# Seven-product up projection of an encoder trunk on one Trainium2 core: weight sums by accumulating DMAs instead of VectorE additions, with a new order table

## The chip, the core and the metric

The kernel runs on one core of one Trainium2 chip. The time is device microseconds of one launch, from three runs of the kernel before: 1785.74, 1783.72 and 1784.91, median 1784.91 us. One further execution was taken by the hardware profiler; every row below is from that one. The engines are named as in the profile: PE is TensorE (PEld its weight loads), DVE is VectorE, ACT is ScalarE, POOL is GpSimd, SP is SyncE, which only issues DMAs here.

## What is computed

Two requests (512 and 256 tokens, together 768 rows, D = 1024) pass through two layers. Layer 0 mixes tokens with a chunked gMLP, layer 1 with a Hyena convolution; each runs beside a cross-attention, and each layer ends in a ConvFFN. The part that the change touches is the first half of layer 1's ConvFFN:

```
def conv_ffn(x, w_up, conv_w, conv_b, w_down):
    h = x @ w_up
    gate = dwconv3(h[..., :D_FF], conv_w, conv_b)
    return (jax.nn.gelu(gate) * h[..., D_FF:]) @ w_down
```

with `D_FF = 2816`, so `w_up` is 1024 x 5632. Everything is float32; a product is made of three single products of a high and a low part (`mm3`: high by high, high by low, low by high).

## The kernel before

**Work and its order.** The program is written as one list of instructions by class `Order` (line 92 on). `schedule` plays that list through with a cost for every instruction and a latency for every hand-over between engines, and emits the instructions engine by engine in the order of that play. Among instructions that could start, the one with the lowest rank goes first; the rank is the instruction's place in the program plus an entry of the table `BIAS` (line 42), which is looked up by the part of the program (`up1`, `out1h1`, ...) and the kind (`pe`, `ve` for DVE, ACT and POOL, `dma`, `load` for whatever serves a weight load). On the chip each engine then runs its own list strictly in order and waits on semaphores for the others. All instructions go through one helper line, so the profile names line L365 for nearly all of them and the groups are told apart by the names of tiles.

**Buffers.** Tiles of 4 KB a partition share 27 places (`s4`). On top of that each kind has a limit of its own: `WR = 4` tiles for raw weights (`wr`, and `wt`, the sums), `WS = 10` tiles for split weights (`ws`). A tile can be filled once one of the places of its kind has been given back by the last reader of an older tile. `wload`, which serves the other projections, takes its raw tile from the same four places.

**Layer 1's up projection** (`ffn_seven`, part `up1`). The 22 blocks of 128 columns are taken in 11 pairs. For each pair `seven` is called twice, once for the gate columns (tiles `g`) and once for the others (tiles `u`): 22 calls. A call makes the four products of two column blocks with two token halves and two halves of the contraction by seven products instead of eight (the Strassen-Winograd scheme), each of 4 x 3 matmuls of 128x384, 84 matmuls a call. The seven right sides are the tiles `x`, made once by `seven_of` from three pairs of token tiles when layer 1's output projection is done (part `out1h1`). The seven left sides come from `seven_weights`: two raw tiles R1 and R2 of 128x1024 (a column block each; half a is the first half of the contraction, half b the second), of which products 1 and 2 use the halves of R1 as they are, product 3 uses R2's half b, and

- product 5 uses R1a + R2a,
- product 6 uses R1a + R2a + R2b,
- product 7 uses R2a + R2b,
- product 4 uses R1a + R1b + R2a + R2b.

Before, DVE makes those with four additions of 128x512 (`wt<-wr`, `wt<-wt,wr`, `wr<-wr`, `wr<-wt,wr`), two of them in place in R2 and R1, so a call holds three of the four raw places. Each weight tile is then split: ACT copies it to the high part, DVE subtracts that from it for the low part. A call fills seven `ws` tiles. The raw tiles are loaded by SP. SP's list also holds the stores of the gated rows (`hsp<-gate`), which wait for DVE.

**The output projection before it** (`out_proj`, part `out1`, its second half `out1h1`) finishes one tile of 128 tokens after the other, in the order 0, 3, 1, 4, 2, 5. Each tile is normed (`rpost`, `rstd` on POOL; `xr`, `y` on DVE; squares on ACT), and each pair goes through `seven_of`: four differences on DVE (`sd`, `se`), transposes on PE (`tps`), and the split of `x` on ACT and DVE. POOL does only such small statistics and a few memsets; it runs nothing in the up projection.

Of the kernel before, what the change touches and what calls it, by code (L numbers as in the profile page):

```python
# [13 lines left out]
F32 = mybir.dt.float32  # L14
# [3 lines left out]
ALU = mybir.AluOpType  # L18
# [15 lines left out]
B8, B4 = 14, 27  # L34
T4, WR, WS, M8, M4 = 9, 4, 10, 14, 22
# [3 lines left out]

AHEAD = 427  # L40
BIAS = {
    ('', 'dma'): -2,
    ('att0', 'pe'): -316, ('att0', 've'): -260,
    ('att1', 'pe'): -14, ('att1', 've'): -1384,
    ('block0', 'pe'): -163, ('block0', 've'): -39,
    ('block1', 'load'): 340, ('block1', 'pe'): -167, ('block1', 've'): 145,
    ('block2', 'load'): 1617, ('block2', 've'): -9,
    ('conv', 'dma'): 560, ('conv', 'pe'): -564, ('conv', 've'): -528,
    ('down0', 'load'): 958, ('down0', 'pe'): 163,
    ('down0h0', 've'): -4337,  # L50
    ('down0h1', 'dma'): 2296, ('down0h1', 'pe'): 305, ('down0h1', 've'): -207,
    ('down1', 'load'): 1243, ('down1', 'pe'): -12,
    ('down1h0', 've'): 261,
    ('down1h1', 'dma'): 293, ('down1h1', 've'): -320,
    ('filters', 'dma'): 790, ('filters', 'pe'): 146, ('filters', 've'): 1331,
    ('gate', 'dma'): 137, ('gate', 'pe'): -8, ('gate', 've'): 289,
    ('kv0', 'dma'): -214, ('kv0', 'load'): 897, ('kv0', 'pe'): -937,
    ('kv1', 'dma'): -395, ('kv1', 'load'): -76, ('kv1', 'pe'): -858, ('kv1', 've'): 21,
    ('mixed', 'pe'): -486, ('mixed', 've'): 124,
    ('normv', 've'): -1344,  # L60
    ('out0', 'load'): 532, ('out0', 'pe'): -124,
    ('out0h0', 've'): -1398,
    ('out0h1', 'dma'): 1199, ('out0h1', 'pe'): 67, ('out0h1', 've'): -313,
    ('out1', 'load'): 13, ('out1', 'pe'): -143,
    ('out1h0', 've'): 816,
    ('out1h1', 'dma'): -336, ('out1h1', 'pe'): -113, ('out1h1', 've'): -391,
    ('pre', 'dma'): -1178, ('pre', 'load'): -660, ('pre', 'pe'): -165,
    ('presplit', 'dma'): -820, ('presplit', 've'): -839,
    ('q0', 'pe'): 232, ('q0', 've'): -564,
    ('q1', 'load'): 1748, ('q1', 'pe'): 140, ('q1', 've'): 123,  # L70
    ('rows', 'load'): -821, ('rows', 'pe'): 293, ('rows', 've'): 294,
    ('up0', 'pe'): -154, ('up0', 've'): -1419,
    ('up1', 'dma'): -300, ('up1', 'load'): 324, ('up1', 'pe'): 61, ('up1', 've'): -419,
    ('x2', 'load'): -53, ('x2', 'pe'): -34, ('x2', 've'): 159,
}
LN_EPS = 1e-5
ATT_SCALE = 0.125
# [15 lines left out]
class Order:  # L93
# [57 lines left out]
    def add(self, eng, method, args, kw):  # L151
        i = len(self.ops)
        outs = [kw[k] for k in ("out", "accum_out") if isinstance(kw.get(k), bass.AP)]
        ins = [v for k, v in kw.items() if isinstance(v, bass.AP) and k not in ("out", "accum_out")]
        pos = [v for v in args if isinstance(v, bass.AP)]
        if "out" not in kw:
            outs, ins = outs + pos[:1], ins + pos[1:]
        else:
            ins += pos
        deps, after, tiles = set(), set(), []  # L160
        for write, aps in ((False, ins), (True, outs)):
            for ap in aps:
                name = ap.tensor.name
                dram = ap.space == bass.MemoryType.DRAM
                if dram and name not in self.state:
                    if name not in self.dram:
                        continue
                st = self.state.setdefault(name, ([], []))
                p0, p1, m = self.region(ap)
                if ap.space == bass.MemoryType.PSUM:  # L170
                    p0, p1, m = 0, 128, 1
                for lst in (st if write else st[1:]):
                    for o, e, q0, q1, mm in lst:
                        if p0 < q1 and q0 < p1 and m & mm:
                            deps.add(o)
                if write:
                    for n in range(2):
                        st[n][:] = [x for x in st[n] if not (p0 <= x[2] and x[3] <= p1 and x[4] & ~m == 0)
                                    or x[0] == i]
                    st[1].append((i, eng, p0, p1, m))  # L180
                else:
                    st[0].append((i, eng, p0, p1, m))
                t = self.tiles.get(name)
                if t is not None and t["ops"] and t["ops"][0] != i:
                    after.add(t["ops"][0])
                if t is not None and (not t["ops"] or t["ops"][-1] != i):
                    t["ops"].append(i)
                    tiles.append(name)
        deps.discard(i)
        kind = "load" if self.load else {"tensor": "pe", "sync": "dma"}.get(eng, "ve")  # L190
        self.rank.append(i + BIAS.get((self.part, kind), 0))
        self.ops.append((eng, method, args, kw, deps, tiles, self.cost(eng, method, kw, args, outs, ins), after - deps))

    @staticmethod
    def cost(eng, method, kw, args, outs, ins):
        n = max(int(np.prod([c for s, c in x.ap[1:]])) for x in outs)
        psum = any(x.space == bass.MemoryType.PSUM for x in ins)
        if eng == "tensor":
            if method == "transpose":
                return 110  # L200
            if kw["rhs"].dtype == F32R:
                return 13.5 + n / 2.4 if n >= 256 else 229
            return 20 + 4 * n / 2.4
        if eng == "scalar":
            c = (52 if psum else 95) + 0.833 * n
            return c + (190 if isinstance(kw.get("bias"), bass.AP) or isinstance(kw.get("scale"), bass.AP) else 0) + \
                (90 if "accum_out" in kw else 0)
        if eng == "vector":
            if method in ("tensor_scalar", "tensor_copy") and not psum:
                return 68 + 0.522 * n  # L210
            if method == "tensor_reduce" or method == "bn_stats":
                n = max(int(np.prod([c for s, c in x.ap[1:]])) for x in ins)
            return (130 if method == "scalar_tensor_tensor" else 69) + 1.042 * n
        if eng == "gpsimd":
            return 300 + 1.1 * n if method == "memset" else 600
        return 450


    def schedule(self):
        ops, N = self.ops, len(self.ops)  # L220
# [69 lines left out]
        while oldest < N:  # L290
            best = None
            for e, c in pool.items():
                pick, at = None, None
                skipped = 0
                for i in sorted(c, key=self.rank.__getitem__):
                    if i > oldest + AHEAD:
                        continue
                    t = allowed(i)
# [10 lines left out]
            at, i, e = best  # L309
            pool[e].remove(i)  # L310
            c = ops[i][6]
            if e == "sync":
                ap = ops[i][3]["out"]
                n = 4 * ap.ap[0][1] * int(np.prod([x[1] for x in ap.ap[1:]]))
                start = max(dma_free, at + 1100)
# [20 lines left out]
            for name in ops[i][5]:  # L336
                t = self.tiles[name]
                left[name] -= 1
                t["end"] = max(t["end"], finish[i])
                if left[name] == 0:  # L340
                    for tag, b in t["res"]:
                        ahead[tag].discard(pos[name, tag])
                        free[tag].append(t["end"] + (900 if e == "sync" else 200))
            while oldest < N and done[oldest]:
                oldest += 1
            for tag in ahead:
# [2 lines left out]
            for u, whole in users[i]:  # L349
                if not whole:  # L350
                    ready_t[u] = max(ready_t[u], at + 1)
                lat = self.LAT[e][ops[u][0]]
                if whole:
                    ready_t[u] = max(ready_t[u], finish[i] + lat)
                need[u] -= 1
                if need[u] == 0:
                    pool[ops[u][0]].append(u)
# [70 lines left out]
class Prog:  # L428
# [146 lines left out]
    def seven_weights(self, ap1, ap2):  # L575

        with self.nc.of(load=True):
            R1, R2, T = (self.nc.tile(self.p4, [128, 1024], F32, "s4", B4, n, n, WR) for n in ("wr", "wr", "wt"))
            self.nc.sync.dma_start(out=R1, in_=ap1)
            self.nc.sync.dma_start(out=R2, in_=ap2)  # L580
            a, b = slice(0, 512), slice(512, 1024)
            W = {}

            def split(src, *ms):
# [2 lines left out]
                for m, q in zip(ms, (a, b)):  # L587
                    W[m] = h[:, q], l[:, q]
            split(R1, 1, 2)
            self.tt(T[:, a], R1[:, a], R2[:, a], ALU.add)  # L590
            self.tt(T[:, b], T[:, a], R2[:, b], ALU.add)
            split(T, 5, 6)
            self.tt(R2[:, a], R2[:, a], R2[:, b], ALU.add)
            split(R2, 7, 3)
            self.tt(R1[:, a], T[:, b], R1[:, b], ALU.add)
            w = self.ws([128, 2, 512])
            self.split(w[:, 0], w[:, 1], R1[:, a])
            W[4] = w[:, 0], w[:, 1]
            return W

    def seven(self, ap1, ap2, xc, name):
# [861 lines left out]
```

## Time and profile before

| | |
|---|---|
| median of three runs | 1784.91 us (1783.72 to 1785.74) |
| time of the profiled execution | 1784.29 us |
| its span in the profile | 1782.5 us |
| mean granted PE clock | 0.992 of full |
| PE busy | 1745.7 us, 98% of the span |
| DVE busy | 1143.0 us, 64% |
| ACT busy | 696.3 us, 39% |
| POOL busy | 82.2 us, 5% |
| DMA traffic | 236.19 MB, mean 133 GB/s |

Layer 1's up projection takes the stretch from about 1268 to 1588 us of the span. A time in the profile is counted from the start of the span; "busy" is the time in which at least one instruction of that engine ran. PE's matmuls overlap one another, so the durations of single matmuls add up to more than PE's busy time. In a timeline row, the bracket says how long the engine had been idle before and which engine's result ended that idle time.

### The profile page before, as it was taken

How to read it: one execution, taken by the hardware profiler on the slowest of the kernel's cores; microseconds unless marked ns; L12 is line 12 of the kernel's file. 1: busy time of each engine (PE TensorE's matmuls, PEld its weight loads, DVE VectorE, ACT ScalarE, POOL GpSimd, SP SyncE). 2: the span in 40 equal slices, each digit the busy share in tenths (PEclk: the TensorE clock that was granted, in tenths of full speed). 3: DMA queues.
4: the chain of work that ended last, by engine and by line, in shares of the span. 5: the costliest groups of instructions: out<-in, count | busy, mean ns of one | idle time of the engine just before them, and what ended most of it. 6: DMA issues, size and time to landing. Idle time of an engine off the chain costs nothing.

```text
span 1782.5 us, 23756 instructions
## 1 busy us (share of the span) xinstructions
PE 1745.7 (98%) x9504; PEld 1542.9 (87%) x9504; DVE 1143.0 (64%) x1675; ACT 696.3 (39%) x1075; POOL 82.2 (5%) x165
## 2 busy tenths in 40 slices
PE   7999999999999999999999999999799999999998
PEld 6988878888888888888798888888699999998886
DVE  6464456456545666663656989764988888874352
ACT  6373344333323334552441222554454443443320
POOL 2001020000000000000300000001100000000001
PEclk9999999999999999999999999999799999999999
DMA  7112044122323135786753324123323232356522
GB/s 268 60 65 95 24 171 139 38 97 75 118 90 114 66 134 220 292 315 219 252 213 118 118 83 131 36 95 118 107 77 127 73 127 77 131 209 224 195 81 106
DMA packets 66830, 236.19 MB, mean 133 GB/s; under 512 B 7475, under 2 KB 7679, under 8 KB 64160
## 3 DMA queue, kind: packets, MB, share of 16 engines
q1 hardware_dynamic: 66720, 234.68, 37.4%
q8 instruction: 75, 1.23, 0.3%
q14 instruction: 35, 0.29, 0.1%
HBM read 183.00 MB, written 51.64 MB: 132 GB/s over the span
## 4 chain that ended last, share of the span: by engine, by line
PE 93%; DVE 5%; DMA 1%; issue 1%; ACT 1%; POOL 1%; POOLq 0%; SPq 0%; DVEq 0%; ACTq 0%
PE rp L365 32%; PE fmp L365 10%; PE fma L365 10%; PE fmb L365 10%; PE bQ L365 8%; PE bA L365 5%; PE bP L365 5%; PE dft L365 3%; PE iv L365 1%; PE kps L365 1%; PE vps L365 1%; PE tps L365 1%; PE h L365 1%; PE sc L365 1%; PE pv L365 1%; DVE x L365 1%
## 5 line engine op out<-in xcount | busy, mean ns | idle before, releaser
L365 PE MATMUL fmp<-hTP,ws 128*128 128x256 f32 x1584 | 405.4, 286 | 0.0
L365 DVE TENSOR_TENSOR ws<-wr,ws 128x1024 fp32r<-128x1024 f32 (+1 forms) x192 | 219.7, 1158 | 118.0 <-ACT ws L365 79.6
L365 PE MATMUL fma<-hTS,ws 128*128 128x512 f32 x792 | 290.1, 398 | 1.6 <-DVE hTS L365 0.8
L365 PEld LDWEIGHTS fmp<-hTP,ws 128*128 128x128 f32 x1584 | 288.4, 190 | 3.1 <-issue 1.1
L365 PE MATMUL fmb<-hTS,ws 128*128 128x512 f32 x792 | 290.9, 399 | 0.0
L365 PE MATMUL bQ<-x,ws 128*128 128x384 f32 x792 | 247.6, 334 | 0.0
L365 ACT ACTIVATE ws<-wr 128x1024 fp32r<-128x1024 f32 (+1 forms) x192 | 189.4, 1004 | 147.7 <-DMA wr<-w_up 68.4
L365 PE MATMUL rp<-ws,xs 128*128 128x512 f32 x792 | 185.1, 389 | 0.0
L365 PEld LDWEIGHTS fma<-hTS,ws 128*128 128x128 f32 x792 | 148.8, 188 | 35.0 <-ACT hTS L365 1.4
L365 PEld LDWEIGHTS fmb<-hTS,ws 128*128 128x128 f32 x792 | 148.8, 188 | 33.3
L365 PE MATMUL bP<-x,ws 128*128 128x384 f32 x528 | 176.4, 334 | 0.0
L365 PEld LDWEIGHTS rp<-ws,xs 128*128 128x128 f32 x792 | 148.6, 188 | 30.8
L365 PE MATMUL bA<-x,ws 128*128 128x384 f32 x528 | 171.5, 343 | 1.2 <-DVE x L365 0.8
L365 PEld LDWEIGHTS bQ<-x,ws 128*128 128x128 f32 x792 | 147.1, 188 | 0.3
L365 PE MATMUL rp<-ws,xsS 128*128 128x512 f32 x528 | 136.9, 390 | 0.0
L365 PE MATMUL rp<-ws,mxS 128*128 128x512 f32 x384 | 117.2, 406 | 0.2 <-DVE ws L365 0.2
L365 PEld LDWEIGHTS rp<-ws,xsS 128*128 128x128 f32 x528 | 99.0, 188 | 20.8
L365 PEld LDWEIGHTS bA<-x,ws 128*128 128x128 f32 x528 | 100.5, 192 | 2.4 <-DVE x L365 1.3
L365 PEld LDWEIGHTS bP<-x,ws 128*128 128x128 f32 x528 | 99.1, 188 | 0.2
L365 PEld LDWEIGHTS rp<-ws,mxS 128*128 128x128 f32 x384 | 71.0, 188 | 15.8 <-DVE ws L365 0.5
L365 PE MATMUL rp<-ws,hTS 128*128 128x512 f32 x288 | 83.8, 403 | 0.0
L365 DVE TENSOR_TENSOR xs<-hc,xs 128x1536 fp32r<-128x1536 f32 x22 | 38.6, 1758 | 64.6 <-ACT ws L365 36.6
(255 smaller groups left out, 2695.2 us busy)
## 6 DMA issues: line engine op xcount, KB each, us to landing
wr<-w_up SPq DMA_DIRECT2D x88, 512.0 KB
wr<-w_down SPq DMA_DIRECT2D x44, 512.0 KB
wsp<-pw SPq DMA_DIRECT2D x20, 1024.0 KB
ws<-wsp SPq DMA_DIRECT2D x40, 512.0 KB
hc<-hsp SPq DMA_DIRECT2D x44, 384.0 KB
xs<-xr SPq DMA_DIRECT2D x18, 512.0 KB
praw<-bw SPq DMA_DIRECT2D x18, 512.0 KB
xr<-xs SPq DMA_DIRECT2D x18, 512.0 KB
```

The lines of the kernel that those rows point to most:

```text
L365: getattr(getattr(self.real, eng), method)(*args, **kw)
```

## The change

`seven_weights` makes the sums by DMAs that add to their destination. It takes a fourth tile U, and SP loads four half tiles more per call (R1a into T's half a, R2b into T's half b, R2a into U's half a, R1b into U's half b). Then POOL issues four DMAs from SBUF to SBUF that add: R2a to T's a (product 5), R2b to U's a (product 7), T's a to T's b (product 6), T's b to U's b (product 4). T and U are split as whole tiles, and product 3 is split from R2's half b. The four additions on DVE are gone; the splits are the same in number and size. In `Order`, a DMA that adds counts its destination as an input too, one issued by POOL is costed at 1200 ns of POOL, and its transfer and hand-over like those of a DMA of SP. `BIAS` has new values in nearly all entries, and some entries come and go.

```
 BIAS = {
...
-    ('out1', 'load'): 13, ('out1', 'pe'): -143,
-    ('out1h0', 've'): 816,
-    ('out1h1', 'dma'): -336, ('out1h1', 'pe'): -113, ('out1h1', 've'): -391,
...
+    ('out1', 'load'): -182, ('out1', 'pe'): 289,
+    ('out1h0', 've'): 539,
+    ('out1h1', 'dma'): -1929, ('out1h1', 'pe'): -1500, ('out1h1', 've'): 126,
...
-    ('up1', 'dma'): -300, ('up1', 'load'): 324, ('up1', 'pe'): 61, ('up1', 've'): -419,
-    ('x2', 'load'): -53, ('x2', 'pe'): -34, ('x2', 've'): 159,
...
+    ('up1', 'dma'): -257, ('up1', 'load'): 194, ('up1', 'pe'): -6, ('up1', 've'): 554,
+    ('x2', 'pe'): -24,
 }
...
+        if kw.get("accum_op") is not None:
+            ins.append(kw["out"])
...
+        if eng == "gpsimd" and method == "dma_start":
+            return 1200
...
-            if e == "sync":
+            if e == "sync" or ops[i][1] == "dma_start":
...
-                lat = self.LAT[e][ops[u][0]]
+                lat = self.LAT["sync" if ops[i][1] == "dma_start" else e][ops[u][0]]
...
     def seven_weights(self, ap1, ap2):
         with self.nc.of(load=True):
-            R1, R2, T = (self.nc.tile(self.p4, [128, 1024], F32, "s4", B4, n, n, WR) for n in ("wr", "wr", "wt"))
-            self.nc.sync.dma_start(out=R1, in_=ap1)
-            self.nc.sync.dma_start(out=R2, in_=ap2)
+            R1, R2, T, U = (self.nc.tile(self.p4, [128, 1024], F32, "s4", B4, n, n, WR)
+                            for n in ("wr", "wr", "wt", "wt"))
             a, b = slice(0, 512), slice(512, 1024)
+            put = self.nc.sync.dma_start
+            for o, i in ((R1, ap1), (R2, ap2), (T[:, a], ap1[:, a]), (T[:, b], ap2[:, b]), (U[:, a], ap2[:, a]),
+                         (U[:, b], ap1[:, b])):
+                put(out=o, in_=i)
+            add = lambda o, i: self.nc.gpsimd.dma_start(out=o, in_=i, accum_op=ALU.add)
+            add(T[:, a], R2[:, a])
+            add(U[:, a], R2[:, b])
+            add(T[:, b], T[:, a])
+            add(U[:, b], T[:, b])
             W = {}
...
             split(R1, 1, 2)
-            self.tt(T[:, a], R1[:, a], R2[:, a], ALU.add)
-            self.tt(T[:, b], T[:, a], R2[:, b], ALU.add)
             split(T, 5, 6)
-            self.tt(R2[:, a], R2[:, a], R2[:, b], ALU.add)
-            split(R2, 7, 3)
-            self.tt(R1[:, a], T[:, b], R1[:, b], ALU.add)
+            split(U, 7, 4)
             w = self.ws([128, 2, 512])
-            self.split(w[:, 0], w[:, 1], R1[:, a])
-            W[4] = w[:, 0], w[:, 1]
+            self.split(w[:, 0], w[:, 1], R2[:, b])
+            W[3] = w[:, 0], w[:, 1]
             return W
```

## Rows read from the trace of the kernel before

**Rows 1.** The page, part 1: busy time of each engine.

```profile
PE 1745.7 (98%) x9504; PEld 1542.9 (87%) x9504; DVE 1143.0 (64%) x1675; ACT 696.3 (39%) x1075; POOL 82.2 (5%) x165
```

**Rows 2.** Stretches of 50 us: busy PE, PEld, DVE, ACT, POOL; clock; DMA share; GB/s.

```profile
750.00:800.00 50.00, 50.00 (x222) 41.43 (x221) 33.61 (x35) 28.50 (x40) 2.18 (x2) 1.00 0.88 324
...
1200.00:1250.00 50.00, 46.73 (x221) 38.38 (x219) 24.92 (x34) 19.09 (x40) 8.21 (x19) 1.00 0.30 106
1250.00:1300.00 50.00, 39.40 (x207) 37.45 (x208) 46.98 (x69) 26.08 (x41) 6.57 (x11) 0.80 0.31 106
...
1350.00:1400.00 50.00, 50.00 (x290) 49.99 (x289) 42.44 (x64) 21.73 (x30) 0.00 (x0) 1.00 0.26 87
```

**Rows 3.** Short stretches inside the transition, the same columns.

```profile
1250.00:1255.00 5.00, 0.20 (x1) 0.20 (x2) 5.00 (x8) 2.30 (x4) 2.39 (x4) 0.55 0.52 210
...
1270.00:1275.00 5.00, 5.00 (x20) 4.88 (x19) 4.32 (x7) 2.12 (x2) 0.00 (x0) 0.56 0.49 184
1275.00:1280.00 5.00, 5.00 (x37) 4.83 (x36) 3.81 (x6) 3.30 (x7) 0.00 (x0) 1.00 0.00 0
```

**Rows 4.** Timeline of PE in the transition.

```profile
1254.80 1.97 PE L365 MATMUL tps<-ident,y 128*128 128x128 f32 x8 [8.04 <-DVE y L365]
...
1265.40 1.94 PE L365 MATMUL tps<-ident,y 128*128 128x128 f32 x8 [4.05 <-DVE y L365]
1267.82 1.01 PE L365 MATMUL bA<-x,ws 128*128 128x384 f32 x2 [0.47 <-ACT x L365]
1269.57 4.85 PE L365 MATMUL bA<-x,ws 128*128 128x384 f32 x14 [0.75 <-DVE x L365]
```

**Rows 5.** Timeline of DVE at the start of the up projection.

```profile
1263.98 1.28 DVE L365 SCALAR_TENSOR_TENSOR y<-xr,rstd,gpre 128x1024 f32<-128x1024 f32 x1
...
1267.09 0.69 DVE L365 TENSOR_TENSOR wt<-wr 128x512 f32<-128x512 f32 x1
1267.70 1.22 DVE L365 TENSOR_TENSOR ws<-wr,ws 128x1024 fp32r<-128x1024 f32 x1
1268.83 1.28 DVE L365 TENSOR_TENSOR x<-tps,x 128x512 fp32r<-128x512 f32 x2
1270.03 0.68 DVE L365 TENSOR_TENSOR wt<-wt,wr 128x512 f32<-128x512 f32 x1
...
1271.83 0.69 DVE L365 TENSOR_TENSOR wr<-wr 128x512 f32<-128x512 f32 x1
```

**Rows 6.** Timeline of POOL in the transition; the last row is POOL's last before 1750.

```profile
1253.69 1.10 POOL L365 TENSOR_SCALAR rstdm<-ss 128x1 f32<-128x1 f32 x1 [0.72 <-ACT y L365]
1254.88 0.94 POOL L365 TENSOR_TENSOR rstd<-rstdm,half 128x1 f32<-128x1 f32 x1
...
1269.16 0.55 POOL L365 TENSOR_TENSOR rstd<-rstdm,half 128x1 f32<-128x1 f32 x1
```

**Rows 7.** Instructions on the sums: ns min/median/max, first and last start.

```profile
L365 DVE TENSOR_TENSOR wt<-wr x22: 681/684/693, 1267.1 to 1564.2; 128x512 f32<-128x512 f32 x22
L365 DVE TENSOR_TENSOR wt<-wt,wr x22: 682/689/694, 1270.0 to 1565.2; 128x512 f32<-128x512 f32 x22
L365 ACT ACTIVATE ws<-wt x22: 1052/1061/1064, 1270.7 to 1565.9; 128x1024 fp32r<-128x1024 f32 x22
L365 DVE TENSOR_TENSOR ws<-wt,ws x22: 1215/1219/1227, 1279.3 to 1576.3; 128x1024 fp32r<-128x1024 f32 x22
```

**Rows 8.** Timeline of SP in the up projection, one pair to the next.

```profile
1366.70 2.12 SPq L365 DMA_DIRECT2D hsp<-gate  x2
1368.93 10.49 SPq L365 DMA_DIRECT2D wr<-w_up  x4
1395.65 2.12 SPq L365 DMA_DIRECT2D hsp<-gate  x2
```

**Rows 9.** Timeline of DVE in that pair: first sum of a call.

```profile
1374.49 0.69 DVE L365 TENSOR_TENSOR wt<-wr 128x512 f32<-128x512 f32 x1 [0.71 <-DMA wr<-w_up]
```

**Rows 10.** Timeline of SP at the span's start: the first load.

```profile
0.73 0.39 SPq L365 DMA_DIRECT2D x<-x  x1
```

**Rows 11.** Timeline of ACT at the span's start: the first user of that load.

```profile
4.53 1.06 ACT L365 ACTIVATE hn<-x 128x1024 f32<-128x1024 f32 x1 [2.52 <-DMA x<-x]
```

**Rows 12.** Timeline of SP in that pair, from 1370.5 on: second and third load.

```profile
1370.36 0.85 SPq L365 DMA_DIRECT2D wr<-w_up  x2
```

More of the change, by code (lines that the diff above doesn't have):

```diff
@@ L41 @@
 BIAS = {
[L42 to L60, printed above, removed]
@@ L61 @@
-    ('out0', 'load'): 532, ('out0', 'pe'): -124,
-    ('out0h0', 've'): -1398,
-    ('out0h1', 'dma'): 1199, ('out0h1', 'pe'): 67, ('out0h1', 've'): -313,
-    ('out1', 'load'): 13, ('out1', 'pe'): -143,
-    ('out1h0', 've'): 816,
-    ('out1h1', 'dma'): -336, ('out1h1', 'pe'): -113, ('out1h1', 've'): -391,
[L67 to L70, printed above, removed]
@@ L71 @@
-    ('rows', 'load'): -821, ('rows', 'pe'): 293, ('rows', 've'): 294,
-    ('up0', 'pe'): -154, ('up0', 've'): -1419,
-    ('up1', 'dma'): -300, ('up1', 'load'): 324, ('up1', 'pe'): 61, ('up1', 've'): -419,
-    ('x2', 'load'): -53, ('x2', 'pe'): -34, ('x2', 've'): 159,
+    ('', 'dma'): 734,
+    ('att0', 'pe'): -778, ('att0', 've'): -802,
+    ('att1', 'pe'): -200, ('att1', 've'): -447,
+    ('block0', 'pe'): -170, ('block0', 've'): -709,
+    ('block1', 'load'): -1027, ('block1', 'pe'): -593, ('block1', 've'): 854,
@@ new lines @@
+    ('block2', 'load'): 1239, ('block2', 'pe'): -573, ('block2', 've'): -2238,
+    ('conv', 'dma'): 298, ('conv', 'pe'): -318, ('conv', 've'): -69,
+    ('down0', 'load'): 1501, ('down0', 'pe'): 151,
+    ('down0h0', 've'): 1815,
+    ('down0h1', 'pe'): 305, ('down0h1', 've'): -457,
+    ('down1', 'load'): 16, ('down1', 'pe'): -146,
+    ('down1h0', 've'): 242,
+    ('down1h1', 'dma'): 238, ('down1h1', 've'): 461,
+    ('filters', 'dma'): 2, ('filters', 'pe'): 91, ('filters', 've'): 1291,
+    ('gate', 'dma'): -148, ('gate', 'pe'): -8, ('gate', 've'): 544,
@@ new lines @@
+    ('kv0', 'dma'): -11, ('kv0', 'load'): -12, ('kv0', 'pe'): -507, ('kv0', 've'): -196,
+    ('kv1', 'dma'): -377, ('kv1', 'load'): 28, ('kv1', 'pe'): -717, ('kv1', 've'): -640,
+    ('mixed', 'pe'): -446, ('mixed', 've'): 360,
+    ('normv', 've'): 11,
+    ('out0', 'load'): -1059, ('out0', 'pe'): -125,
+    ('out0h0', 've'): 1631,
+    ('out0h1', 'pe'): 58, ('out0h1', 've'): -543,
+    ('out1', 'load'): -182, ('out1', 'pe'): 289,
+    ('out1h0', 've'): 539,
+    ('out1h1', 'dma'): -1929, ('out1h1', 'pe'): -1500, ('out1h1', 've'): 126,
@@ new lines @@
+    ('pre', 'dma'): -1379, ('pre', 'load'): -32, ('pre', 'pe'): -410, ('pre', 've'): -767,
+    ('presplit', 'dma'): 381, ('presplit', 've'): 787,
+    ('q0', 'load'): 465, ('q0', 'pe'): -428, ('q0', 've'): -470,
+    ('q1', 'load'): -1318, ('q1', 'pe'): 146, ('q1', 've'): 580,
+    ('rows', 'load'): 149, ('rows', 'pe'): 300, ('rows', 've'): 49,
+    ('up0', 'load'): -545, ('up0', 'pe'): 29, ('up0', 've'): 920,
+    ('up1', 'dma'): -257, ('up1', 'load'): 194, ('up1', 'pe'): -6, ('up1', 've'): 554,
@@ L342, in schedule @@
                         ahead[tag].discard(pos[name, tag])
-                        free[tag].append(t["end"] + (900 if e == "sync" else 200))
+                        free[tag].append(t["end"] + (900 if ops[i][1] == "dma_start" else 200))
             while oldest < N and done[oldest]:
```

## The prediction

> **What bounds the kernel now.** I read the busy times of the page first [rows 1]: PE is busy for 1745.7 of 1782.5 us, so every other engine can matter only through the 36.8 us in which PE is idle, or through the clock. Then the stretches of 50 us [rows 2]. In a stretch of the up projection, 1350 to 1400, PE is busy for 50.00 of 50 us, its weight loads for 49.99, at full clock, and makes 290 matmuls: 0.1724 us each. A call of 84 matmuls is thus 14.48 us, and the SP timeline shows the same: the stores that close a pair of calls start 28.95 us apart [rows 8]. DVE is busy for 42.44 of those 50 us; it has 15% to spare, and PE never waits for it there. So the stage in which the change works has no idle time of PE to give back. The only large loss nearby is the transition before it: from 1200 to 1300 PE idles for 3.27 and 10.60 us [rows 2], while DVE is busy for 46.98 of the second 50, and the granted clock is 0.55 or 0.56 of full, the lower of the two levels, in 1250 to 1255 and 1270 to 1275, and full again after 1275 [rows 3]; PE had idled for 8.04 us before 1254.80 and for 4.05 us before 1265.40 [rows 4]. DVE bounds that transition.
>
> **The change part by part.** *DVE additions removed.* Four a call, 22 calls, 0.69 us each [rows 7]: 88 x 0.69 = 61 us of DVE. In steady state they are worth nothing, since PE is full; what hides them is PE's own matmuls. In the transition three of them come early enough to be looked at, at 1267.09, 1270.03 and 1271.83 [rows 5]. The first pushes the split of the weights and the two `x` behind it by 0.61 us (1267.09 to 1267.70), and PE waits 0.75 us for such an `x` before 1269.57 [rows 4]. I take 0.6 us gained; the bounds are 0 and 1.2 us (both waits of PE, 0.47 and 0.75). The other two fall where PE is busy for 5.00 of 5 us [rows 3], so they gain nothing. The last `y` that PE idles for is made at 1263.98, ahead of all three [rows 5], so the big gaps keep their length.
>
> *Loads added.* Four a call, 88 in all, 256 KB each. SP issues two loads in 0.85 us [rows 12], so 1.7 us of SP in a call of 14.48. They are queued, like the loads now, behind the two stores that wait for DVE's gating (2.12 us for the two, [rows 8]). Who waits for that is the adds. Hidden, as long as the sums are early; the cost if not is rival C.
>
> *Adds on POOL.* 88 issues. No row shows one. For POOL's own time I take 1.1 us, the longest of the small instructions in its timeline [rows 6]: 4.4 us a call. In the up projection POOL has 0.00 us of other work [rows 2], so nothing stands behind an add but the next add. For the time x from one add's issue until its sum can be used, the nearest rows are plain loads. The first 512 KB load was issued at 0.73 [rows 10] and its reader began at 4.53, after a wait ended by that DMA [rows 11]: 3.8 us. At the 324 GB/s that the busiest stretch moved [rows 2], 256 KB less are 0.8 us less: 3.0 us for a plain load of the size of an add. Lower bound of x: the issue of 0.39 us and 0.8 us of data, 1.2 us. Upper bound: 3.0, a second passage of the data (0.8), POOL's 1.1: 4.9 us. I take 3.0 + 0.8 = 3.8 us, since an add must read two operands and its issue lies inside the 3.0 of the row. The Trainium skill (DMA: Bandwidth & Descriptors, section Anatomy of one DMA) has a fit for DMAs of this issuer, 2.0 us plus the bytes at 436 GB/s; by it x would be an estimated 2.6 us and the loop below 11.6 us. No run here shows it.
>
> *Are the sums in time?* All four raw places belong to one call now, so the next call's T can be loaded only when a tile of this call is given back. If T follows T and U follows U, the loop is: load, two adds in a row, split. The load is 4.1 us (issue of the second load at 1370.36, its sum begins at 1374.49 after a wait ended by the DMA [rows 9, 12]). The split is 1.06 on ACT and 1.22 on DVE [rows 7], 2.3 us. Loop: 4.1 + 2 x 3.8 + 2.3 = 14.0 us against a call of 14.48. It fits, by 0.5 us only; at x = 1.2 it is 8.8, at 4.9 it is 16.2. I cost it at nothing, with little confidence.
>
> *Traffic.* At 87 GB/s [rows 2] a call moves 1.26 MB; the loads add 1.05, the adds 1.05, or 2.1 if the destination's reading counts. That makes 232 to 305 GB/s. In 750 to 800 the engines moved 324 GB/s with PE busy for 50.00 [rows 2]. Hidden.
>
> *Removed from ACT and DVE in place:* nothing else; the splits stay. In the old order the sums of R2 and R1 in place delayed the giving back of their tiles; now T and U take that part.
>
> *The new table.* It moves instructions of every stage. What it can win lies in PE's idle time, 36.8 us, of which 13.9 are in 1200 to 1300; what it loses shows nowhere in advance. I take 0, with 6 us to either side: about half of the 13.9, less the change's own 0.6.
>
> **Sum.** The profiled execution took 1784.29 us (span 1782.5 and 1.8 around it), 0.6 below the median of the runs shown. 1784.29 - 0.6 = **1783.7 us**. A measurement of this kernel can tell about 0.2%, 3.6 us: faster is below 1781.3, slower above 1788.5.
>
> **Rivals.**
> *A, forecast:* the sums are hidden, PE stays full, 1783.7; with the table's 6 us its own range is 1778 to 1790.
> *B, the transition shortens.* With no sums in DVE's list the new order lets DVE serve the token tiles without a break and PE has work for half of the 13.9 idle us: 7 us, 1777. For it: DVE is full there (46.98 of 50) and the ranks of `out1h1` and `up1` move apart. Against it: up to 1267 DVE's list in that stretch holds no sum, so the work that PE waits for is as long as before.
> *C, slower: the loop of the raw tiles is longer than a call.* It decides from x = 4.0 us on (4.1 + 2.3 + 2x = 14.48), or from 2.7 us if T has to wait for the older U, as then three adds stand in the loop. At x = 4.9 each of 21 calls loses 1.7 us: 36 us, 1820. With three adds at x = 3.8 the loop is 17.8, 3.3 us a call, 70 us, 1854. For it: the margin is 0.5 us, the loads come in bursts of six, and gaps of 4 and 8 us brought the clock to its lower level in the transition [rows 3, 4], though gaps of 2 us a call need not. Against it: now the loads are issued so that the sums start 0.71 us after the wait begins [rows 9] and still PE is full, so splits stand well ahead of their matmuls. The same page of the Trainium skill (section Issuing engines are not separate DMA queues) says that DMAs of all issuers run on the same 16 engines and interleave; by that rule the adds lengthen the loads in the loop, which speaks for C. The DMA share of 0.88 in 750 to 800 beside a full PE is what this trace has on it, and it does not show such a loop.
> *D, slower: the first call's adds stand in POOL's list among the statistics of the last token tiles.* There an add that waits for the one before it holds back `rstd` (1253.69 to 1269.16 [rows 6]), which `y` and so PE wait for. One x of 3.8 us, partly at half clock: some 6 us, 1790. It decides where an add is issued between 1244 and 1269 before its data are there. Against it: POOL has nothing to do for hundreds of us before, so the adds can stand earlier.
>
> **How the numbers follow.** A 0.55: the margin is positive at the middle value of x, and the tiles most likely follow their own kind. Of A, 0.20 lie below 1781.3, 0.27 within, 0.08 above. B 0.13. C 0.26, since a third of the span between the bounds of x lies near or over its point. D 0.06. Faster 0.20 + 0.13 = 0.33; same 0.27; slower 0.08 + 0.26 + 0.06 = 0.40. The likeliest case is A, so the time is 1783.7. The range runs from 1776 to 1830: it leaves out about half of B with the lower tail of A (0.08) and a third of C (0.09).
>
> **What would show it.** Right: in the stretches from 1300 to 1550 PE stays at 50.00 of 50 with 290 matmuls, DVE falls from 42 to about 34 us (4 x 0.6 us from start to start, 3.45 calls), the DMA rate is above 230 GB/s, pairs stay 28.95 us apart, and the first `bA` starts within a us or two of 1267.8. C right: pairs further apart than 28.95 us, PE waiting for `ws`, ACT waiting for `wt` ended by a DMA of POOL. D right: `rstd` late behind an add. B right: PE idle from 1200 to 1300 well under 13.9 us. Wrong altogether: the difference lies in a stage without weight sums, by the table alone, and by more than 6 us.

## The result and the profile after

The changed kernel takes 1794.91 us (median of 9 runs), the kernel before 1784.91; the ratio is 1.0057, 95% interval 1.0042 to 1.0071. It is slower, by some 10 us, where no difference was forecast, and its runs lie far apart: 1789.50 to 1800.22, against 1783.72 to 1785.79 before. The profiled execution, 1789.50, is the quickest of the nine, so its trace shows less of the loss than most runs have: 5.2 us of span (1787.7 against 1782.5). Its mean granted clock is 0.993 of full, that of the two longest runs 0.988.

PE's busy time in three stretches, cut at the same places in both profiles, says where it went. First before, then after (columns as in [rows 2]):

```profile
0.00:1200.00 1200.00, 1185.03 (x6589) 1024.23 (x6590) 750.37 (x1143) 466.47 (x769) 60.91 (x117) 1.00 0.39 135
1200.00:1300.00 100.00, 86.13 (x428) 75.83 (x427) 71.90 (x102) 45.17 (x81) 14.78 (x30) 0.90 0.30 106
1300.00:1590.00 290.00, 290.00 (x1671) 289.66 (x1671) 238.28 (x358) 126.07 (x164) 0.00 (x0) 1.00 0.31 107
```

```profile
0.00:1200.00 1200.00, 1187.71 (x6612) 1029.00 (x6613) 757.38 (x1148) 468.74 (x773) 63.04 (x117) 1.00 0.39 135
1200.00:1300.00 100.00, 77.18 (x394) 66.97 (x393) 62.47 (x86) 43.97 (x76) 28.58 (x46) 0.91 0.73 198
1300.00:1590.00 290.00, 288.67 (x1655) 286.45 (x1654) 188.53 (x273) 121.37 (x156) 63.09 (x72) 1.00 0.88 231
```

Up to 1200 PE idles 2.7 us less than before: that is the table, as its run below shows. In the transition it idles 22.8 us instead of 13.9, and in the up projection it loses 1.3 us and makes 16 matmuls fewer. Idle time in a stretch cut at a fixed place is not yet lost time, since the work in it has moved; the matmuls made by then count the work. By 1300 PE has made 6589 + 428 = 7017 before and 6612 + 394 = 7006 after: 11 fewer, some 2 us. DVE is relieved as planned, from 238 to 189 us in the up projection. The price is on POOL, 63 us where there was nothing, and on the DMA engines: their share rises from 0.31 to 0.88 at 231 GB/s. Before, 324 GB/s took the same 0.88 [rows 2], so these bytes are dearer.

The page's queues and the issues of the sums, after (packets, MB, share of 16 engines' span; then KB each and median us from issue to landing):

```profile
q0 software_dynamic: 12672, 23.07, 7.6%
...
wt<-wr POOLq DMA_DIRECT2D x44, 256.0 KB, 5.4
wt<-wt POOLq DMA_DIRECT2D x44, 256.0 KB, 5.5
```

An add takes 5.4 us from issue to landing. The forecast had 3.8 until its sum can be used, with 4.9 as the upper bound. ACT, which splits the sums, waits for them in the up projection (1300 to 1590; us, times, longest):

```profile
ACT ws L369 <- DMA wt<-wt: 59.9, 22, 6.8
```

POOL's timeline in the transition, after, answers to [rows 6]:

```profile
1249.69 0.86 POOL L369 DMA_DIRECT2D wt<-wt  x1 [2.76 <-DMA wt<-wr]
...
1257.88 0.89 POOL L369 DMA_DIRECT2D wt<-wr  x1 [4.02 <-DMA wt<-w_up]
1258.93 0.87 POOL L369 DMA_DIRECT2D wt<-wt  x1 [0.16 <-issue]
1259.50 0.66 POOL L369 TENSOR_TENSOR rpostm<-s,s 128x1 f32<-128x1 f32 x2
...
1266.77 1.30 POOL L369 TENSOR_SCALAR rstdm<-ss 128x1 f32<-128x1 f32 x1 [4.90 <-ACT y L369]
```

ACT's timeline in the same stretch:

```profile
1257.11 0.22 ACT L369 ACTIVATION_READ_ACCUMULATOR y<-rp 128x1 f32 x1
...
1264.58 1.06 ACT L369 ACTIVATE ws<-wt 128x1024 fp32r<-128x1024 f32 x1 [0.86 <-DMA wt<-wt]
1265.55 1.04 ACT L369 ACTIVATE y<-xr 128x1024 f32<-128x1024 f32 x1
```

ACT had the squares of the last two token tiles at 1257.3, but POOL stood at an add that waited 4.02 us for its loads, and took up `rpostm` at 1259.50. Later ACT stood 0.86 us at the split of a sum that had not landed, with the squares of `xr` behind it. On PE the first `bA` begins at 1275.1, where before it began at 1267.82 [rows 4]; the last begins 5.1 us later than before, at 1592.4 against 1587.3:

```profile
L369 PE MATMUL bA<-x,ws x528: 333/334/444, 1275.1 to 1592.4; 128*128 128x384 f32 x176
```

### The profile page after: what moved, and what is told of

Same layout as the page of the kernel before. It is cut to its first block, busy times and chain, and to the rows that moved or that the text cites. A ratio compares the mean times of both kernels' runs of the same rounds, so it can differ in the third digit from the quotient of the medians.

```text
span 1787.7 us, 24187 instructions
## 1 busy us (share of the span) xinstructions
PE 1743.3 (98%) x9504; PEld 1540.4 (86%) x9504; DVE 1094.7 (61%) x1587; ACT 696.1 (39%) x1073; POOL 161.2 (9%) x253
## 4 chain that ended last, share of the span: by engine, by line
PE 91%; DMA 3%; issue 2%; DVE 2%; POOL 1%; ACT 1%; SPq 0%; POOLq 0%; DVEq 0%; ACTq 0%
PE rp L369 31%; PE fmp L369 10%; PE fma L369 10%; PE fmb L369 10%; PE bQ L369 6%; PE bA L369 4%; PE bP L369 4%; PE dft L369 4%; PE iv L369 2%; DMA wt<-wt 1%; PE kps L369 1%; PE vps L369 1%; PE sc L369 1%; PE pv L369 1%; PE h L369 1%
## 5 line engine op out<-in xcount | busy, mean ns | idle before, releaser
L369 PE MATMUL fmp<-hTP,ws 128*128 128x256 f32 x1584 | 425.5, 289 | 0.0
L369 PEld LDWEIGHTS fmp<-hTP,ws 128*128 128x128 f32 x1584 | 293.9, 190 | 3.5 <-issue 1.1
L369 PE MATMUL bQ<-x,ws 128*128 128x384 f32 x792 | 253.5, 335 | 0.1
L369 DVE TENSOR_TENSOR ws<-wr,ws 128x1024 fp32r<-128x1024 f32 (+1 forms) x170 | 193.5, 1152 | 91.7 <-PE rp L369 32.5
L369 ACT ACTIVATE ws<-wr 128x1024 fp32r<-128x1024 f32 (+1 forms) x170 | 166.7, 999 | 173.4 <-PE fmp L369 78.8
L369 PE MATMUL rp<-ws,xsS 128*128 128x512 f32 x528 | 147.8, 390 | 0.0
L369 PE MATMUL rp<-ws,mxS 128*128 128x512 f32 x384 | 111.3, 400 | 0.0
L369 PE MATMUL rp<-ws,xsP 128*128 128x512 f32 x264 | 88.2, 399 | 0.0
```

The lines of the kernel that those rows point to most:

```text
L369: getattr(getattr(self.real, eng), method)(*args, **kw)
```

## The experiments

Three causes could share the 10 us: the new table, the adds in the transition, and the adds in the up projection. The first four runs set out to take them apart. Each pairs a table with a mix of instructions that it was not made for, which can cost time of its own (the run without sums below).

**The new table alone.** `BIAS` of the changed kernel in the kernel before.

> The kernel before with the new BIAS table alone; sums stay on VectorE. If the loss lies in the table: about 1790 to 1795 us, as in the changed kernel. If it lies in the adds, in the transition (POOL's and ACT's lists held up there) or in the up projection (loop of the raw tiles longer than a call): at or below the kernel before, 1780 to 1785 us, since up to 1200 us PE idled 2.7 us less in the changed kernel than before; PE idle from 1200 to 1300 about 14 us, runs within 2 us of one another.

1786.31 us, ratio 1.0006 (0.9997 to 1.0014): no difference. Up to 1200 PE idles 2.7 us less than before, and in the transition it is busy for 81.40 of 100 us:

```profile
0.00:1200.00 1200.00, 1187.73 (x6612) 1028.97 (x6613) 756.99 (x1148) 468.74 (x773) 62.42 (x117) 1.00 0.39 135
1200.00:1300.00 100.00, 81.40 (x417) 72.46 (x417) 69.59 (x98) 43.01 (x75) 15.87 (x30) 0.88 0.32 111
```

Of the 8.9 us that PE idles more in the transition after the change, 4.7 are there with the table alone (86.13 to 81.40). But they are not lost there: by 1300 PE has made 6612 + 417 = 7029 matmuls, 12 more than before. What the table has won goes later: PE makes 1662 matmuls from 1300 to 1590, where it made 1671, and idles 1.7 us from 1590 to 1640, where before it was full. Runs lay 2.5 us apart.

**The adds alone.** The changed kernel with the old table.

> The changed kernel with the old BIAS table: the accumulating DMAs alone. If the table is the cause: about 1785 us. If the adds are: 1790 to 1800 us, runs 5 us or more apart, a median add still about 5.4 us from issue to landing.

1822.48 us, ratio 1.0211 (1.0198 to 1.0225): 37 us slower than before, and worse than expected. The new table does not cause the loss, it takes most of it back. In the up projection PE is busy for 275.62 of 290 us, and ACT waits 61.9 us for sums of POOL. How much of the 37 us is the adds' this run does not tell, since the old table was not made for them.

**Adds from the fifth call on.**

```
     def seven_weights(self, ap1, ap2):
+        self.calls = getattr(self, "calls", 0) + 1
+        if self.calls <= 4:
+            return self.seven_weights_dve(ap1, ap2)
```

(`seven_weights_dve` is the function of the kernel before.)

> The changed kernel, but the first 4 of the 22 calls make their sums on VectorE as before; calls 5 to 22 by accumulating DMAs. Transition theory (adds among the statistics in POOL's list, splits that wait for them in ACT's): PE idle from 1200 to 1300 falls from 22.8 us to about 14, time about 1785 to 1787 us. Loop theory (an add takes 5.4 us, loop 4.1 + 2 x 5.4 + 2.3 = 17.2 us against a call of 14.48): the runs stay 5 us or more apart and the median stays over 1790.

1799.30 us, ratio 1.0077 (1.0057 to 1.0097), runs from 1793.25 to 1807.11. The transition is that of the table alone (81.22 of 100 us), and yet the kernel is no faster than the changed one: with adds in the up projection alone it is 14 us slower than before, and the time differs from run to run by as much. No run with copies in these calls tells how much of that is the adding. The profiled execution (1804.82) shows it, PE's stretch and ACT's longest wait there (us, times, longest):

```profile
1300.00:1590.00 290.00, 277.92 (x1567) 275.34 (x1566) 182.86 (x268) 118.72 (x153) 63.94 (x72) 0.98 0.85 221
```

```profile
ACT ws L369 <- DMA wt<-wt: 46.7, 12, 6.0
```

PE makes 104 matmuls fewer there than before (1567 against 1671), some 18 us; 12 of them are idle time, and the granted clock is 0.98 of full in the mean, 0.95 from 1450 to 1500. ACT, in order, waits for late sums up to 6.0 us at a time; behind those splits stand its copies of `bA` out of PSUM, and PE's single longest wait there is 4.4 us for such a copy.

**Adds in the first four calls alone.** The same with `self.calls > 4`.

> The reverse: accumulating DMAs in the first 4 calls alone, VectorE sums in calls 5 to 22. Transition theory: PE idle from 1200 to 1300 stays near 22 us, time 1788 to 1792, runs within 3 us. Loop theory: 1783 to 1786 us, since the loop has no time to fall behind in 4 calls.

1792.53 us, ratio 1.0039 (1.0027 to 1.0051), runs within 3.6 us. PE is busy for 76.78 us in the transition and 289.28 of 290 after. With adds in four calls the kernel is 6.2 us slower than with the table alone. Both halves lose, then, and their losses don't add up: the changed kernel loses 10 us, the two halves 14 and 7.4. Why not was not tried; an order that fits neither half is one possible reason.

**Plain copies.** What is it about an add: POOL's issue, the traffic, or the adding?

```
-            add = lambda o, i: self.nc.gpsimd.dma_start(out=o, in_=i, accum_op=ALU.add)
+            add = lambda o, i: self.nc.gpsimd.dma_start(out=o, in_=i)
```

> The changed kernel with the four DMAs of POOL as plain copies, without adding (the sums of products 4 to 7 are left out; same instructions, bytes written and order). If it is the adding that makes an add slow: issue to landing falls from a median of 5.4 us to 3 to 4, DMA share in the up projection from about 0.9 to under 0.75, PE full from 1300 to 1590, time 1786 to 1790 us (the transition's part stays). If it is POOL's issue, or the crowd of loads: still about 5 us, share about 0.9, time over 1790.

1785.68 us, ratio 1.0004 (0.9995 to 1.0013): the whole loss is gone, with the same 88 DMAs from POOL, the same loads and bytes written, the same order of the lists. The slowest of its 11 runs, 1787.81, is quicker than the quickest of the changed kernel, 1789.50. POOL's instructions on the sums and their landing, min/median/max, with copies:

```profile
L369 POOL DMA_DIRECT2D wt<-wr x44: 536/536/742, 1223.2 to 1567.3; - x44
...
DMA to landing us min/median/max: 2.2/3.0/7.1
```

Its queue on the page, its transition and up projection, and ACT's wait for the copies in the latter:

```profile
q0 software_dynamic: 7040, 23.07, 3.4%
```

```profile
1200.00:1300.00 100.00, 80.20 (x396) 69.65 (x395) 62.36 (x85) 43.46 (x76) 24.01 (x46) 0.88 0.57 195
1300.00:1590.00 290.00, 289.99 (x1671) 289.47 (x1670) 191.15 (x279) 122.08 (x157) 38.72 (x72) 1.00 0.69 234
```

```profile
ACT ws L369 <- DMA wt<-wt: 8.6, 4, 3.5
```

The same view of the changed kernel's adds:

```profile
L369 POOL DMA_DIRECT2D wt<-wr x44: 852/1044/1432, 1221.3 to 1568.8; - x44
...
DMA to landing us min/median/max: 3.3/5.4/10.2
```

A copy lands after 3.0 us, an add after 5.4. A copy is 7040 / 88 = 80 packets and takes 3.4% of 1786 us / 88 = 0.69 us of all 16 engines; an add is 144 packets and 7.6% of 1787.7 us / 88 = 1.54 us, 2.2 times as much for the same bytes. That lifts the engines' share from 0.69 to 0.88 at 234 and 231 GB/s. With little other traffic (engine share 0.38 and 0.32 from 1246 to 1250) the gap is smaller: the next instruction of POOL, which waits for the DMA at 1246, begins 3.66 us after it with an add (1246.03 to 1249.69) and 2.62 us with a copy (1245.73 to 1248.35). The run takes away at once all in which an add differs from a copy: POOL's longer issue, the later landing and the engines' time. It does not tell which of them costs.

It does tell what in the transition is not the adding. POOL's timeline there, and the `bA` on PE, with copies:

```profile
1255.91 0.61 POOL L369 DMA_DIRECT2D wt<-wr  x1 [2.34 <-DMA wt<-w_up]
1257.93 0.55 POOL L369 DMA_DIRECT2D wt<-wt  x1 [1.40 <-DMA wt<-w_up]
1258.49 0.34 POOL L369 TENSOR_TENSOR rpostm<-s,s 128x1 f32<-128x1 f32 x2
...
L369 PE MATMUL bA<-x,ws x528: 334/334/669, 1275.7 to 1590.8; 128*128 128x384 f32 x176
```

POOL stands 2.34 and 1.40 us for the same loads and takes up `rpostm` 1.0 us earlier than with adds, but the first `bA` is as late, 1275.7 against 1275.1, and by 1300 PE has made 6604 + 396 = 7000 matmuls, no more than the 7006 with adds. So the late start of the traced run comes with the added loads and with the places of POOL's DMAs in the lists, and by the median with copies it costs next to nothing. What the adding changes between these two traces is the up projection: ACT waits 59.9 us there and not 8.6, and PE makes 16 matmuls fewer. But the two profiled executions, the quickest with adds and one of the slowest with copies, are only 1.7 us apart (1789.50 and 1787.81); where the rest of the 9.2 us between the medians lies was not traced.

**The same, in the first four calls.** The run with adds in those alone, its adds made plain copies.

> As the run with accumulating DMAs in the first 4 calls alone (1792.5 us), but POOL's DMAs there are plain copies (the sums of those 4 calls are left out). If the slow adding is what costs in the transition: 1785 to 1787 us. If it is their place in POOL's list and the loads of four more half tiles: still 1790 to 1793 us.

1788.47 us, ratio 1.0020 (1.0011 to 1.0029): between the two expectations. Of 7.4 us over the kernel before, 4.0 go with the adding; 3.4 stay with the places in the lists, the loads and the table. Here the adding does delay the start: the first `bA` begins at 1277.9 with adds and at 1273.7 with copies.

**An order made with the true latency.**

```
-                finish[i] = start + n / 360.0
+                finish[i] = start + n / 360.0 + (2700 if e == "gpsimd" else 0)
```

> The changed kernel, with the planner counting 2.7 us more until the sum of an add can be used (issue to use 5.5 us, as measured, in place of 2.7). If the loss comes from an order made for adds that are too quick (in-order lists that wait for a late add): PE idle from 1200 to 1300 falls from 22.8 to 19 or less, and the gaps in the up projection shrink, time 1784 to 1788 us. If four raw tiles are too few for adds of 5.4 us in any order (loop 17.2 us against 14.48): the up projection stays short of work, 1792 us or more.

1794.66 us, ratio 1.0043 (1.0030 to 1.0057): as the changed kernel. The runs are closer (1791.49 to 1795.22), PE idles 21.4 us in the transition instead of 22.8, and the up projection still has gaps. Telling the planner how late the sums are does not cure it, with a table that was not made anew for it; the time is that of the second expectation. This run does not tell whether the tiles or the engines are short.

**Six raw tiles.** `WR = 6`.

> The changed kernel with 6 raw weight tiles in place of 4 (WR = 6; the 27 places they share with all others stay). Loop theory: the next call's loads and adds start earlier, no gaps in the up projection, runs within 3 us, 1785 to 1790 us. If the adds are limited by the DMA engines (share 0.9) and not by the tiles: 1792 us or more, share no lower.

1810.34 us, ratio 1.0141 (1.0127 to 1.0154), and inconclusive: with more raw tiles filled ahead in the places that all tiles share, both the stages before and the transition get worse (PE busy for 6.6 us less up to 1200 than in the changed kernel, first `bA` at 1285.5, PE busy for 75.82 of 100 us). But from 1300 to 1500 PE is busy for 50.00 in every stretch of 50, with adds of 6.0 us median and an engine share of 0.86 to 0.91; the gaps come after 1500. That speaks for the tiles as the shortage, against the engines' share as such.

**Two adds a call.**

```
-            add(T[:, b], T[:, a])
-            add(U[:, b], T[:, b])
+            self.tt(T[:, b], T[:, b], T[:, a], ALU.add)
+            self.tt(U[:, b], U[:, b], T[:, b], ALU.add)
```

> The changed kernel with only the first two sums of a call (products 5 and 7) by accumulating DMAs and the other two (6 and 4) on VectorE, from the same loads. The longest chain in the loop is one add: 4.1 + 5.4 + 0.7 + 2.3 = 12.5 us against a call of 14.48. If the loop decides in the up projection: PE full from 1300 to 1550, runs within 3 us, 1786 to 1792 us (the transition's part may stay). If the DMA engines' load as such decides: gaps of PE there, 1792 us or more.

1791.75 us, ratio 1.0035 (1.0021 to 1.0048), runs 3.5 us apart. An add now lands after 4.1 us (median) at an engine share of 0.66 to 0.73. The time is inside what the loop theory expected, but PE is not full: 47.98 and 48.56 in the stretches from 1300 and from 1400. So neither reading is clean.

**No sums at all.** What could freeing DVE give at best? The additions are left out of the kernel before; products 5 and 6 use R1 again, 7 uses R2a, 4 uses R1b.

```
-            self.tt(T[:, a], R1[:, a], R2[:, a], ALU.add)
-            self.tt(T[:, b], T[:, a], R2[:, b], ALU.add)
-            split(T, 5, 6)
-            self.tt(R2[:, a], R2[:, a], R2[:, b], ALU.add)
+            split(R1, 5, 6)
             split(R2, 7, 3)
-            self.tt(R1[:, a], T[:, b], R1[:, b], ALU.add)
...
-            self.split(w[:, 0], w[:, 1], R1[:, a])
+            self.split(w[:, 0], w[:, 1], R1[:, b])
```

> The kernel before without its four additions on VectorE (the weights of products 4 to 7 are left unsummed, T is left out; all splits and matmuls stay). This is the most that freeing VectorE could ever give with the old table. If the sums cost PE nothing, as the forecast held: 1783 to 1786 us, no difference. If VectorE's relief is worth something in the transition: 1778 to 1782 us.

1800.68 us, ratio 1.0087 (1.0073 to 1.0101). Less work, and 16 us slower; neither expectation has that. The transition is nearly the old one (83.65 of 100 us), but in the up projection PE falls behind, by about half a microsecond at a time: by 1590 it has made 64 matmuls fewer than before, some 11 us, and its weight loads wait 10.9 us there. PE's waits over the whole run (us, times, longest):

```profile
PE bQ L365 <- DVE ws L365: 4.2, 10, 0.6
PE bQ L365 <- DVE u L365: 1.8, 2, 1.4
```

The old entries were made for lists with the four additions in them. Without those, it seems, the planner puts the low parts of the splits so close to their matmuls that each is a little late; that was not tried further.

**No sums, the new table.**

> The same with the new table: what the changed kernel would be with sums that cost nothing on any engine. If the new table was made for a VectorE without sums and is right for it: 1778 to 1782 us. If table and relief are both worth nothing that can be measured: 1783 to 1787 us.

1785.39 us, ratio 1.0003 (0.9994 to 1.0012). The new table serves a DVE without sums, and then the kernel stands where it stood before. So free sums are worth nothing under this table, and the changed kernel pays 9.5 us more for its sums than nothing (1794.91 against 1785.39); the run with copies, at 1785.68, puts that on the adding. A table made for this mix was not tried. With the old table a kernel without any add already loses 16 us, so the 37 us above can't be put on the adds alone.

**Half of each table.** The new entries for all parts up to layer 1's mixer, the old ones for `out1`, `up1` and `down1`; sums on DVE.

> No accumulating DMA: the kernel before with the new BIAS entries for all parts up to the mixer of layer 1, and the old entries for out1, up1 and down1. The new table idled PE 2.7 us less before 1200 us and, alone, 4.7 us more from 1200 to 1300. If the two parts of the table can be taken apart: 1781 to 1783 us, faster than both. If the gain before 1200 is lost again in the transition: 1784 to 1787 us.

1785.21 us, ratio 0.9999 (0.9990 to 1.0008). PE is busy for 42.33 of 50 us from 1200 on, as with the whole new table. What is won before 1200 is lost again: in the transition PE waits 18.5 us for `y` of DVE (12.6 before) and its lead shrinks from 24 matmuls at 1200 to 6 at 1300, and from 1590 to 1640 it idles 1.7 us, where before it was full. No version of the study is faster than the kernel before.

## Why the prediction was wrong

**Right.** Freeing DVE is worth nothing in the up projection: with the sums left out and the new table, 1785.39 us. In the five stretches of 50 us from 1300 to 1550 of the changed kernel's profile DVE is busy for 31.6 to 35.3 us (34 was forecast); DMA moves 220 to 257 GB/s, where 230 and more were forecast. POOL's issue of plain copies and the loads cost nothing that can be measured: with those the kernel is at 1785.68. The table's effect is nothing in sum, inside its 6 us. The plain transfer of 256 KB was estimated at 3.0 us from the first load, and a copy from POOL lands after 3.0. That the two are the same is partly luck: the estimate was for a load by SP at the start of the span, up to its reader; copies by POOL took 2.62 us up to their reader in the quiet stretch, and 2.2 to 7.1 to landing among the loads. The Trainium skill's fit for that issuer (DMA: Bandwidth & Descriptors, Anatomy of one DMA) gave an estimated 2.6 us: near the copies' 2.2 to 3.0, far from the adds' 5.4.

**Wrong: the time of an add among the loads, and with it the nothing for late sums.** The step "3.0 + 0.8 = 3.8 us" took an add for a copy with a second passage of its bytes at 324 GB/s, the copy from the first load of the span. Measured, the adding costs 1.0 us in a quiet stretch (3.66 against 2.62), not far from the 0.8, but 2.4 us among the loads (5.4 against 3.0). The upper bound of 4.9 did not hold the median either, and the case that was called likeliest hung on a margin of 0.5 us. Under "Traffic", the same error: 232 to 305 GB/s were held harmless beside a stretch at 324, but an add takes 1.54 us of all 16 engines where a copy takes 0.69, so the share rose to 0.88. Bytes per second did not measure how busy the engines were. So "Are the sums in time?", costed at nothing, came out at 59.9 us of waits for sums on ACT in the quickest run, and the adding at 9.2 us of the kernel's time (1794.91 against 1785.68). PE did not stay full either: from 1300 to 1550 its stretches hold 290, 277, 287, 290 and 289 matmuls, and the stores of the pairs start 24.9 to 37.4 us apart, not 28.95. The chances had slower at 0.40, ahead of faster and same; the time followed the one likeliest case, A, and 1794.91 lies outside A's own range of 1778 to 1790.

**Rival C held in kind, not in size.** Late sums hold up the in-order lists in the up projection: ACT waits for `wt` ended by DMAs of POOL, the sign that was written down. From which x on was not tried. Its formula gives at x = 5.4 a loop of 4.1 + 10.8 + 2.3 = 17.2 us, 2.7 us in each of 21 calls, 57 us; measured are 1.3 us in the changed kernel's profile, at most some 12 in its slowest run if the whole spread of 10.7 lies there, and 14 us in the run with adds from the fifth call on, whatever part of those the ill-fitting order has. It would fit that the tiles do not follow their own kind so strictly, or that splits that stand ahead of their matmuls absorb part; neither was tried. How the rest divides between four raw tiles and busy engines stays open: the run with six tiles points to the tiles, and the run with two adds has gaps though its loop was reckoned shorter than a call; neither is clean.

**Rival D took place too, and not by the adding alone.** An add among the last statistics held POOL for 4.02 us, waiting for its loads, as in D's condition. The argument against it, that POOL is free for hundreds of microseconds before, did not hold: SP issued the last two loads of the output projection's weights from 1203.44 on and the first of the up projection's at 1213.59, so POOL, idle for 322 us until then, had its first add at 1221.27 and the second call's adds among the statistics. The first `bA` came 7 us late, not within one or two. D had been given 0.06 and 6 us. But with plain copies POOL is held too, for 2.34 and 1.40 us, the first `bA` is as late, and the kernel takes 1785.68. So D's event can come without D's price. What the adding puts on top of it is not the same everywhere: nothing in the changed kernel's traced run, its quickest, but 4.0 us where the first four calls alone are changed (1792.53 against 1788.47).

**Rival B did not happen.** In no variant does PE idle less from 1200 to 1300 than the 13.9 us before; it idles for 16.4 to 24.2 us.

## What to carry to other kernels

Work taken off an engine that was not the bound bought nothing here, 61 us of it; it could only be paid for. An accumulating DMA is no copy: before replacing an addition of 0.69 us by one, measure its time to landing among the real traffic, and count its engine time and not its bytes. And an order table belongs to the instruction mix that it was made for: compare a change under a table made for it, and the new table without the change. To tell a slow instruction from its place in the lists, replace it by a quick one in the same place, as the run with copies does.

## What the runs showed of the hardware that was not expected

An add of 256 KB from SBUF to SBUF is 144 packets where a copy is 80, and POOL is busy with its issue for 0.87 us (`wt<-wt`) or 1.04 us (`wt<-wr`, medians) where a copy takes 0.54. The changed kernel's nine runs also lie 10.7 us apart, those with plain copies 4.0 (11 runs), those with no sums and the new table 2.0 (11 runs). Adds alone don't make that spread: the five runs with the true latency in the planner, with as many adds, lie 3.7 apart. And loads beside them land later: a 512 KB load of `w_up` takes 3.8 us (median) without sums, 4.4 beside copies and the half-tile loads that come with them, 4.6 beside adds. The Trainium skill (DMA: Bandwidth & Descriptors, Issuing engines are not separate DMA queues) says that DMAs of all issuers interleave on the same engines; these numbers agree.
